# Mean squares of a mixer step's input: from token-major tiles with ACT accumulators instead of folds over feature-major squares

## The chip, the cores and the metric

One core of a Trainium2 chip runs the whole step. The metric is device microseconds (us) of one execution, the median of three runs. Engines are called as the profile calls them: PE (TensorE), DVE (VectorE), ACT (ScalarE), POOL (GpSimd), SP (SyncE, which here only issues transfers).

## The reference

One decoder layer over 2,112 tokens (2,048 of a prompt, 64 of samples) with 1,024 features, in float32. What bears on the change is the norm and the projection ahead of everything:

```python
def rms_norm(x, g):
    y = xf * lax.rsqrt(jnp.mean(xf * xf, axis=-1, keepdims=True) + NORM_EPS)
    return (y * g.astype(jnp.float32)).astype(x.dtype)
...
    xn = rms_norm(x, norm_pre)
    z = jnp.einsum('btd,de->bte', xn, w_in.astype(xn.dtype))
    v_pool = z[:, :, 0:W_POOL]
    g_pool = z[:, :, W_POOL:2 * W_POOL]
    ...
    y_pool, new_pool = pool_mixer(v_pool, pool_buf, start_pos, pool_w, pool_scale)
```

So each token needs one number, the reciprocal root of the mean square of its 1,024 features. After that come a pooling mixer with a gate, a convolution with a gated linear recurrence and its gate, an output projection, a second norm and the residual.

## The kernel before, in words

Tokens are cut into five chunks of up to 426 columns (`CHUNKS`; c = 0 to 4). The normalised input of all chunks stays in SBUF, features on partitions (feature-major): eight blocks k of 128 features, W columns each, as a high part `xh` and a low part `xl`, both rounded to fp32r. A projection of a chunk (`z_k`) is three matmuls for each k: high weights by `xh`, high weights by `xl`, low weights by `xh`.

The change is in the first stage, pool group 0, which runs under `tc.manual_schedule()` (L596 to L812): each engine takes its instructions in the order in which the code writes them. For every chunk PE computes two value blocks (v0, v1), the group's linear map of the chunk before (`pool_mm`) and two gate blocks (g0, g1), 24 + 24 + 12 + 24 + 24 matmuls. The last chunk has 12 more for its own map; then `fold_mm` starts the next stage.

Chunk 0 is the odd one: its matmuls run on x times the norm's gain (`x_g`, `x_hi`, `x_lo`), and the reciprocal root `r0` comes in afterwards, where DVE takes v0 and v1 out of PSUM (`pool_evac`) and g0 and g1 (L717). For chunks 1 to 4 `normalise` multiplies x in place by gain and root (DVE, L239), ACT rounds the high part (L247) and DVE or POOL subtracts for the low part (L256).

Where the roots come from: ACT squares x feature-major (`square`, L583; L675 for chunk 4, whose blocks are loaded for it in passing and loaded again by `normalise`), `fold` adds the eight blocks of features by halving (4, 2, 1 blocks; on DVE for chunks 0 and 1, on POOL for 2 and 3; `add_parts` on POOL for chunk 4), and one matmul of a 128x128 matrix of ones (`mean_sq`, L211) sums over the partitions and spreads the sum to all of them. ACT takes Ln and Exp (`rsqrt_table`), DVE makes a Newton step on 128 x W elements (`rsqrt_newton`), and the row `r` lies in SBUF. `MS0_AT`, `MS1_AT` and `MS_AT` say behind which k that matmul stands in PE's order. Ln and Exp share a table of ACT that Silu isn't in, so the code loads tables by hand.

All transfers go through SP's queue, in order. SBUF slots of 128 x 3,408 float32 (tag `xn`, ten of them) hold x, `xh`, `xl`, staged weights and the squares.

Of the kernel before, what the change touches and what calls it, by code (L numbers as in the profile page):

```python
# [61 lines left out]
def hymba_kernel(  # L62
# [146 lines left out]
    def mean_sq(c, acc):  # L209
        ms = s_psum(f"ms{c}")[:, :XR[c][1] - XR[c][0]]  # L210
        nc.tensor.matmul(ms, lhsT=ones, rhs=acc, start=True, stop=True)  # L211
        return ms

    def rsqrt_table(ms, r, preload=True):
        if preload:
# [4 lines left out]
    def rsqrt_newton(acc, ms, r):  # L220
        V = nc.vector
        V.scalar_tensor_tensor(out=acc, in0=ms, scalar=D * EPS, in1=r, op0=ALU.add, op1=ALU.mult)
        V.scalar_tensor_tensor(out=acc, in0=acc, scalar=-0.5 / D, in1=r, op0=ALU.mult, op1=ALU.mult)
        V.scalar_tensor_tensor(out=r, in0=acc, scalar=1.5, in1=r, op0=ALU.add, op1=ALU.mult)
# [355 lines left out]
    sqt = {}  # L580

    def square(c, k0, k1):
        A.activation(out=sqt[c][:, k0 * CW:k1 * CW], in_=xraw[c][:, k0 * CW:k1 * CW], func=AF.Square)  # L583

    def fold(c, eng, acc, ns):
        W = XR[c][1] - XR[c][0]
        for n in ns:
            eng.tensor_tensor(out=sqt[c][:, 0:n * W] if n > 1 else acc, in0=sqt[c][:, 0:n * W],
                              in1=sqt[c][:, n * W:2 * n * W], op=ALU.add)
# [6 lines left out]
    with tc.manual_schedule():  # L596
# [55 lines left out]
        square(0, 6, 8)
        acc0 = t_tile("xa0")[:, :CW]
        acc1 = t_tile("xa1")[:, :CW]
        fold(0, V, acc0, (4, 2, 1))
# [2 lines left out]
        square(1, 0, 4)
        square(1, 4, 8)
        half = 2 * CW  # L660
        for eng, o in ((G, 0), (V, half)):
            eng.tensor_tensor(out=sqt[1][:, o:o + half], in0=sqt[1][:, o:o + half],
                              in1=sqt[1][:, 2 * half + o:3 * half + o], op=ALU.add)
        fold(1, V, acc1, (2, 1))
# [3 lines left out]
        def squares(c):
            sqt[c] = half_slot(f"sq{c}", F32)
            square(c, 0, 4)  # L670
            square(c, 4, 8)

        def square_part(k):
            t = x_part(LAST, k)
            A.activation(out=t, in_=t, func=AF.Square)  # L675
            return t
# [828 lines left out]
```

## Time and profile before

| | |
|---|---|
| median of three runs | 1207.81 us (1207.54 to 1207.96) |
| the profiled execution | 1207.61 us, its span 1205.7 us |
| PE busy | 1169.7 us, 97% of the span |
| DVE, ACT, POOL busy | 869.0, 556.0, 391.8 us |
| mean granted clock of PE | 0.991 |
| PE busy in the first four of 40 slices (30 us each), tenths | 6, 8, 8, 7; from the fifth on 9 nearly throughout |

PE works nearly without a break, apart from the first 150 us and the last few. The profile therefore has to be read in the first stage: where PE waits there, for whom, and why that one was late. Times in the rows further down are us from the start of the span.

### The profile page before, as it was taken

How to read it: one execution, taken by the hardware profiler on the slowest of the kernel's cores; microseconds unless marked ns; L12 is line 12 of the kernel's file. 1: busy time of each engine (PE TensorE's matmuls, PEld its weight loads, DVE VectorE, ACT ScalarE, POOL GpSimd, SP SyncE). 2: the span in 40 equal slices, each digit the busy share in tenths (PEclk: the TensorE clock that was granted, in tenths of full speed). 3: DMA queues.
4: the chain of work that ended last, by engine and by line, in shares of the span. 5: the costliest groups of instructions: out<-in, count | busy, mean ns of one | idle time of the engine just before them, and what ended most of it. 6: DMA issues, size and time to landing. Idle time of an engine off the chain costs nothing.

```text
span 1205.7 us, 16176 instructions
## 1 busy us (share of the span) xinstructions
PE 1169.7 (97%) x5762; PEld 1075.1 (89%) x5762; DVE 869.0 (72%) x1209; ACT 556.0 (46%) x986; POOL 391.8 (32%) x498
## 2 busy tenths in 40 slices
PE   6887999999999999999999999999999999999997
PEld 5787999999999999999999999999978878888886
DVE  7899654435545455888888888889976678888687
ACT  5464321221221125676767676677754333344232
POOL 4466530341251152333333334334320002221242
PEclk9899999999999999999999999999999999999999
DMA  9011362543341020111111111112469857767553
GB/s 320 21 44 57 93 211 93 166 141 118 120 159 57 28 62 32 53 43 43 47 37 44 40 53 48 44 40 84 141 196 275 249 168 206 224 190 236 158 164 140
DMA packets 126673, 140.02 MB, mean 116 GB/s; under 512 B 12288, under 2 KB 88320, under 8 KB 126592
## 3 DMA queue, kind: packets, MB, share of 16 engines
q1 hardware_dynamic: 126592, 138.99, 37.7%
q8 instruction: 45, 0.74, 0.3%
q14 instruction: 36, 0.29, 0.1%
HBM read 99.46 MB, written 39.24 MB: 115 GB/s over the span
## 4 chain that ended last, share of the span: by engine, by line
PE 72%; DVE 11%; DMA 8%; ACT 5%; POOL 2%; issue 2%; SPq 0%; DVEq 0%; ACTq 0%; POOLq 0%
PE p L995 6%; PE p L994 6%; PE p L993 6%; PE u L269 5%; PE u L270 5%; PE u L271 5%; PE lg L269 5%; PE lg L270 4%; PE lg L271 4%; PE v L269 3%; PE v L270 3%; PE v L271 3%; PE g L269 3%; PE g L271 3%; PE g L270 3%; DMA a<-mixed 3%
## 5 line engine op out<-in xcount | busy, mean ns | idle before, releaser
L471 DVE SCALAR_TENSOR_TENSOR xs<-u,parT,xs 128x426 f32<-128x426 f32 (+1 forms) x120 | 108.9, 907 | 46.9 <-ACT xs L467 30.7
L270 PE MATMUL v<-xl,w 128*128 128x426 f32 (+2 forms) x320 | 117.7, 368 | 11.0 <-DVE xl L256 8.7
L269 PE MATMUL v<-xh,w 128*128 128x426 f32 (+2 forms) x320 | 118.5, 370 | 7.8 <-ACT xh L574 7.4
L986 POOL TENSOR_TENSOR xr<-ac,xr 128x512 f32<-128x512 f32 x28 | 47.2, 1707 | 230.2 <-DVE ac L1124 126.4
L269 PE MATMUL g<-xh,w 128*128 128x426 f32 (+1 forms) x320 | 115.5, 361 | 3.8 <-ACT e L303 3.8
L271 PE MATMUL v<-xh,w 128*128 128x426 f32 (+2 forms) x320 | 114.5, 363 | 0.0
L269 PE MATMUL u<-xh,w 128*128 128x426 f32 (+1 forms) x320 | 114.0, 356 | 0.0
L270 PE MATMUL g<-xl,w 128*128 128x426 f32 (+1 forms) x320 | 114.0, 356 | 0.0
L271 PE MATMUL g<-xh,w 128*128 128x426 f32 (+1 forms) x320 | 113.9, 356 | 0.1
L269 PE MATMUL lg<-xh,w 128*128 128x426 f32 (+1 forms) x320 | 113.9, 356 | 0.0
L270 PE MATMUL lg<-xl,w 128*128 128x426 f32 (+1 forms) x320 | 113.4, 354 | 0.0
L270 PE MATMUL u<-xl,w 128*128 128x426 f32 (+1 forms) x320 | 113.4, 354 | 0.0
L271 PE MATMUL lg<-xh,w 128*128 128x426 f32 (+1 forms) x320 | 113.4, 354 | 0.0
L271 PE MATMUL u<-xh,w 128*128 128x426 f32 (+1 forms) x320 | 113.2, 354 | 0.0
L1286 DVE RECIPROCAL rv<-rv 128x426 f32<-128x426 f32 (+1 forms) x40 | 112.4, 2811 | 0.0
L993 PE MATMUL p<-ws,s 128*128 128x512 f32 (+1 forms) x264 | 102.3, 387 | 0.7 <-ACT s L106 0.7
L994 PE MATMUL p<-ws,s 128*128 128x512 f32 (+1 forms) x264 | 102.2, 387 | 0.2 <-DVE ws L109 0.2
L995 PE MATMUL p<-ws,s 128*128 128x512 f32 (+1 forms) x264 | 102.3, 388 | 0.0
L270 PEld LDWEIGHTS v<-xl,w 128*128 128x128 f32 x320 | 62.0, 194 | 17.9 <-DVE xl L256 11.3
L994 PE MATMUL p<-ws,a 128*128 128x512 f32 x192 | 75.8, 395 | 0.5 <-DVE ws L109 0.4
L993 PE MATMUL p<-ws,a 128*128 128x512 f32 x192 | 75.7, 394 | 0.5 <-ACT ws L106 0.5
L332 DVE TENSOR_TENSOR s<-e 128x440 f32<-128x440 f32 (+3 forms) x40 | 30.9, 771 | 62.7 <-ACT e L303 49.0
(235 smaller groups left out, 2891.7 us busy)
## 6 DMA issues: line engine op xcount, KB each, us to landing
a<-mixed SPq DMA_DIRECT2D x112, 256.0 KB, 4.3
wr<-in_w_in SPq DMA_DIRECT2D x56, 256.0 KB, 3.1
wo<-in_w_out SPq DMA_DIRECT2D x32, 256.0 KB, 3.8
wtd<-wo SPq DMA_DIRECT2D x32, 256.0 KB, 2.3
w<-wtd SPq DMA_DIRECT2D x32, 256.0 KB, 3.8
xr<-in_x SPq DMA_DIRECT2D x32, 256.0 KB, 3.7
out<-xr SPq DMA_DIRECT2D x30, 256.0 KB, 2.6
mixed<-sg SPq DMA_DIRECT2D x32, 213.0 KB, 2.0
```

Source lines behind the costliest of these rows:

```text
L269: nc.tensor.matmul(out, lhsT=wh, rhs=xh, start=(k == 0), stop=False)
L270: nc.tensor.matmul(out, lhsT=wh, rhs=xl, start=False, stop=False)
L271: nc.tensor.matmul(out, lhsT=wl, rhs=xh, start=False, stop=(k == KT - 1))
L332: nc.vector.tensor_tensor(out=dst[:, first:L], in0=src[:, first:L], in1=src[:, first - sh:L - sh], op=ALU.add)
L471: nc.vector.scalar_tensor_tensor(out=xs, in0=E[:, k:k + n], scalar=col(C_CW + 8 * k, b), in1=xs, op0=ALU.mult, op1=ALU.add)
L986: (eng or nc.vector).tensor_tensor(out=out, in0=a, in1=b, op=op)
L993: nc.tensor.matmul(out, lhsT=ah, rhs=wh, start=start and k == 0, stop=False)
L994: nc.tensor.matmul(out, lhsT=ah, rhs=wl, start=False, stop=False)
L995: nc.tensor.matmul(out, lhsT=al, rhs=wh, start=False, stop=stop and k == KT - 1)
L1286: nc.vector.reciprocal(out=v, in_=v)
```

## The change

x is loaded a second time, token-major: 17 tiles of 128 tokens x 1,024 features (512 KB each, the last one half), three to a slot. ACT squares a tile in place with an accumulator (`tok_square`), which gives the sum of a token's squares in one column of the small tile `tok`. `tok_rsqrt` makes root columns out of sums for several tiles at once (7, 3 and 7 columns): mean and epsilon on DVE, Ln and Exp on ACT, a Newton step on DVE, all on 128 x 3 or 128 x 7 elements. `r_rows` turns the columns of a chunk into a row on all partitions: for each of the four or five tiles that the chunk touches ACT scales columns of an identity matrix by the root column (a diagonal `dg`), and a matmul of ones with it writes the piece into PSUM. There `normalise` reads it; only r0 is copied to SBUF. `R01_AT` and `R_AT` place these matmuls in PE's order. The squares, folds, `add_parts`, the first loads of chunk 4 and all but one table load for Ln go.

```diff
@@ rows of roots
+    tok = sb.tile([P, 3, N_TT], F32, name="tok")
+    def load_tok(i, slot):
+        lo, hi = i * P, min((i + 1) * P, T_ALL)
+        t = tok_box[i] = slot[:hi - lo, i % 3 * D:(i % 3 + 1) * D]
+        nc.sync.dma_start(out=t, in_=x[lo:hi, :])
+    def tok_square(i):
+        t = tok_box[i]
+        nc.scalar.activation(out=t, in_=t, func=AF.Square, accum_out=tok[:t.shape[0], 0, i:i + 1])
+    def tok_rsqrt(i0, i1):
+        V = nc.vector
+        ms, u, r = (tok[:, i, i0:i1] for i in range(3))
+        V.tensor_scalar(out=ms, in0=ms, scalar1=1.0 / D, scalar2=EPS, op0=ALU.mult, op1=ALU.add)
+        nc.scalar.activation(out=r, in_=ms, func=AF.Ln)
         nc.scalar.activation(out=r, in_=r, func=AF.Exp, scale=-0.5)
+        V.tensor_tensor(out=u, in0=ms, in1=r, op=ALU.mult)
+        V.scalar_tensor_tensor(out=u, in0=u, scalar=-0.5, in1=r, op0=ALU.mult, op1=ALU.mult)
+        V.scalar_tensor_tensor(out=r, in0=u, scalar=1.5, in1=r, op0=ALU.add, op1=ALU.mult)
+    def r_rows(c):
+        lo, hi = XR[c]
+        dg = tp_tile(f"dg{c}")
+        R = s_psum(f"r{c}")[:, :hi - lo]
+        for i in range(lo // P, (hi - 1) // P + 1):
+            n = min(P, T_ALL - i * P)
+            a, b = max(lo, i * P), min(hi, i * P + n)
+            nc.scalar.activation(out=dg[:n, a - lo:b - lo], in_=ident[:n, a - i * P:b - i * P], func=AF.Copy,
+                                 scale=tok[:n, 2, i:i + 1])
+            nc.tensor.matmul(R[:, a - lo:b - lo], lhsT=ones[:n, :], rhs=dg[:n, a - lo:b - lo], start=True, stop=True)
+        return R
...
@@ opening: loads
         stage_w(8, 0, 2)
+        for i in range(4):
+            load_tok(i, slots[i // 3])
         load_x(1, 0, 4)
+        for i in range(4, 6):
+            load_tok(i, slots[1])
         load_x(1, 4, 8)
+        load_tok(6, slots[2])
...
@@ opening: ACT, PE and DVE (the squares of chunks 0 and 1 and their folds go)
         w_hi(8, 0, A)
         w_lo(8, 0, G)
+        for i in range(3):
+            tok_square(i)
         w_hi(8, 1, A)
         w_lo(8, 1, G)
+        for i in range(3, 7):
+            tok_square(i)
+        for i in range(7, 9):
+            load_tok(i, slots[2])
         load_x(3, 0, KT)
...
-            if k == MS0_AT:
-                ms0 = mean_sq(0, acc0)
-        rsqrt_table(ms0, r0, False)
-        rsqrt_newton(acc0, ms0, r0)
+        for i in range(9, 12):
+            load_tok(i, slots[1])
+        tok_rsqrt(0, 7)
...
         for k in range(KT):
+            if k == R01_AT:
+                R0, r1 = r_rows(0), r_rows(1)
+                A.copy(out=r0, in_=R0)
             z_k(Z0[3], wt[9], 0, k)
...
-        squares(2)
...
-        accs = {2: sums(2, G)}
-        normalise(1, r1, [V])
+        normalise(1, r1, [V], {3: (7,), 5: (8,), 7: (9,)})
+        for i in range(10, 12):
+            tok_square(i)
+        for i in range(12, 15):
+            load_tok(i, slots[2])
...
@@ chunks 1 to 4
-                r = rsqrt()
+                tok_rsqrt(7, 10)
+                r = r_rows(n)
...
-                squares(3)
-                accs[3] = sums(3, G)
...
-                    if k == MS_AT and n:
-                        r = rsqrt()
+                    if k == R_AT and n:
+                        r = r_rows(n)
...
-                    add_parts()
-                    parts = [square_part(k) for k in range(4, KT)]
-                    add_parts()
...
-                last = normalise(n, r, LO_ENGS[n], SQUARES if c == 1 else {})
+                last = normalise(n, r, LO_ENGS[n], {1: (12,), 3: (13,), 5: (14,)} if c == 1 else {})
             if c == 1:
+                for i in range(15, 17):
+                    load_tok(i, slots[2])
+                    tok_square(i)
+                tok_rsqrt(10, 17)
                 silus()
...
-                nc.scalar.preload_act_table_set("natural_log_exp_and_others")
```

The numbers behind a name tell its buffers apart. Three places show how the order on the engines changes.

SP's queue at the opening, before and then now, from the load of weight block 8 (`wst`, 128x1024) on. `xr_123` and `xr_134` are x of chunk 1, `xr_131` and `xr_144` of chunk 2, `xr_192` and `xr_199` of chunk 3, `w9r` is weight block 9; `tok_108`, `tok_109`, `tok_110` are the three slots of token-major tiles.

```order
L556 DMA wst<-in_w_in 128x1024
L198 DMA xr_123<-in_xt 128x4x426 x2
L611 DMA w9r_91<-in_w_in 128x512
L611 DMA w9r_92<-in_w_in 128x512
L615 DMA pw0r<-in_pool_w 128x512
L198 DMA xr_131<-in_xt 128x8x426
L198 DMA xr_192<-in_xt 128x8x426
```

```order
L578 DMA wst<-in_w_in 128x1024
L220 DMA tok_108<-in_x 128x1024 x3
L220 DMA tok_109<-in_x 128x1024
L202 DMA xr_134<-in_xt 128x4x426
L220 DMA tok_109<-in_x 128x1024 x2
L202 DMA xr_134<-in_xt 128x4x426
L220 DMA tok_110<-in_x 128x1024
L627 DMA w9r_96<-in_w_in 128x512
L627 DMA w9r_97<-in_w_in 128x512
L629 DMA pw0r<-in_pool_w 128x512
L202 DMA xr_144<-in_xt 128x8x426
```

Seven token-major tiles (0 to 6) now stand among and behind the loads of chunk 1 and ahead of weight block 9; tiles 7 to 11 follow chunks 2 and 3.

ACT at the opening, from the cast of weight block 8's first half to the first cast of chunk 1 (`xh_326`, now `xh_341`), before and then now. `w_0_99`, `w_1_100` and now `w_0_104`, `w_1_105` are the two halves of weight block 9.

```order
L562 CAST w_0_97<-wst 128x512
L583 ACTIVATE sq_128<-xr_123 128x1704 x2
L562 CAST w_1_98<-wst 128x512
L217 ACTIVATE r_104<-ms_239,epsT 128x426
L218 ACTIVATE r_104<-r_104 128x426
L562 CAST w_0_99<-w9r_91 128x512
L562 CAST w_1_100<-w9r_92 128x512
L217 ACTIVATE xr_279<-ms_267,epsT 128x426
L218 ACTIVATE xr_279<-xr_279 128x426
L583 ACTIVATE sq_319<-xr_131 128x1704 x2
L247 CAST xh_326<-xr_123 128x426 x2
```

```order
L224 ACTIVATE tok_109,tok<-tok_109 128x1024 x3
L224 ACTIVATE tok_110,tok<-tok_110 128x1024
L230 ACTIVATE tok<-tok 128x7
L231 ACTIVATE tok<-tok 128x7
L584 CAST w_0_104<-w9r_96 128x512
L584 CAST w_1_105<-w9r_97 128x512
L243 ACTIVATE dg_295<-ident,tok 128x128 x3
L243 ACTIVATE dg_295<-ident,tok 128x42
L243 ACTIVATE dg_305<-ident,tok 128x86
L243 ACTIVATE dg_305<-ident,tok 128x128 x2
L243 ACTIVATE dg_305<-ident,tok 128x84
L691 COPY r_111<-r_296 128x426
```

The casts of weight block 9 now stand behind the squares of tiles 0 to 6 and the roots of seven columns; before they stood behind the roots of chunk 0.

ACT in chunk 3, around the roots of chunk 4, before and then now. `xh_101` and `xh_106` are the high parts of chunk 0, which is normalised anew there for the other pool groups.

```order
L805 ACT_TABLE_LOAD
L247 CAST xh_101<-xr_112 128x852 x4
L217 ACTIVATE xr_809<-ms_807,epsT 128x424
L218 ACTIVATE xr_809<-xr_809 128x424
L303 COPY e_3_815<-v_3_781 128x426
L760 ACT_TABLE_LOAD
```

```order
L269 CAST xh_106<-xr_119 128x852 x4
L243 ACTIVATE dg_813<-ident,tok 128x104
L243 ACTIVATE dg_813<-ident,tok 128x128 x2
L243 ACTIVATE dg_813<-ident,tok 64x64
L325 COPY e_3_823<-v_3_787 128x426
```

Before, PE's matmul `ms_807` stood ahead of ACT's work and needed only sums from POOL; now PE's matmuls for chunk 4's row need these four diagonals, which ACT makes behind the four casts.

## Rows read from the trace of the kernel before

**Rows 1.** The waits of PE in the first 165 us: who waited for whom; us in total, how often, longest.

```profile
PE v L270 <- DVE xl L256: 8.7, 4, 3.1
...
PE g L269 <- ACT e L303: 3.8, 1, 3.8
PE ms L211 <- DVE xa L588: 3.3, 1, 3.3
PE v L270 <- POOL xl L256: 1.5, 2, 0.9
...
PE y L284 <- POOL dl L109: 0.7, 1, 0.7
PE f L285 <- POOL wtl L109: 0.5, 1, 0.5
```

**Rows 2.** PE's timeline in the first stage, the matmuls at which blocks begin or waits end: start, duration, line, operation, and in brackets the idle time before it and who ended it. The row of 53.75 is the sum for chunk 2, the next one the start of `pool_mm`; the rows of 66.10, 93.20 and 123.68 begin chunks 2, 3 and 4, the last one the next stage.

```profile
24.05 1.79 PE L211 MATMUL ms<-xa,ones 128*128 128x426 f32 x2 [3.34 <-DVE xa L588]
...
53.75 0.88 PE L211 MATMUL ms<-xa,ones 128*128 128x426 f32 x2
...
59.10 0.35 PE L283 MATMUL y<-dh,pw 128*128 128x426 f32 x1
...
61.44 0.36 PE L269 MATMUL g<-xh,w 128*128 128x426 f32 x1
...
66.10 0.36 PE L269 MATMUL v<-xh,w 128*128 128x426 f32 x1
...
70.91 0.46 PE L270 MATMUL v<-xl,w 128*128 128x426 f32 x1 [3.10 <-DVE xl L256]
...
93.20 0.36 PE L269 MATMUL v<-xh,w 128*128 128x426 f32 x1
...
123.68 0.35 PE L269 MATMUL v<-xh,w 128*128 128x408 f32 x1
...
147.39 0.28 PE L283 MATMUL f<-pw,wth 128*128 128x256 f32 x1
```

**Rows 3.** Stretches of 10 us in the first stage: busy time of PE and its instructions, granted clock of PE (1.00 is 2.4 GHz), share of the DMA engines, GB/s.

```profile
20.00:30.00 10.00, 6.66 (x25) 0.83 0.93 333
40.00:50.00 10.00, 7.79 (x28) 0.66 0.00 0
...
70.00:80.00 10.00, 9.03 (x36) 0.83 0.12 44
90.00:100.00 10.00, 7.86 (x37) 1.00 0.00 0
110.00:120.00 10.00, 7.02 (x30) 0.83 0.11 25
```

**Rows 4.** DVE's timeline between 36 and 110 us, columns as in rows 2.

```profile
36.14 3.84 DVE L256 TENSOR_TENSOR xl<-xr,xh 128x426 fp32r<-128x426 f32 x1 [0.37 <-issue]
39.90 3.66 DVE L239 SCALAR_TENSOR_TENSOR xr<-xr,parT,xr 128x426 f32<-128x426 f32 x2
43.48 0.59 DVE L256 TENSOR_TENSOR xl<-xr,xh 128x426 fp32r<-128x426 f32 x1
...
49.26 1.10 DVE L717 TENSOR_TENSOR sg<-g,r 128x426 f32<-128x426 f32 x2
...
54.03 0.16 DVE L358 TENSOR_TENSOR d<-df,e 128x1 f32<-128x1 f32 x1
...
59.30 2.38 DVE L239 SCALAR_TENSOR_TENSOR xr<-xr,parT,xr 128x426 f32<-128x426 f32 x4
62.04 4.28 DVE L256 TENSOR_TENSOR xl<-xr,xh 128x852 fp32r<-128x852 f32 x1 [0.35 <-ACT xh L247]
...
92.73 4.13 DVE L239 SCALAR_TENSOR_TENSOR xr<-xr,parT,xr 128x426 f32<-128x426 f32 x4
...
101.71 8.78 DVE L239 SCALAR_TENSOR_TENSOR xr<-xr,parT,r 128x426 f32<-128x426 f32 x8
```

**Rows 5.** POOL's timeline in the same time, columns as in rows 2.

```profile
27.68 2.90 POOL L565 TENSOR_TENSOR w<-w9r,w 128x512 fp32r<-128x512 f32 x2 [2.56 <-ACT w L562]
...
35.70 6.14 POOL L588 TENSOR_TENSOR sq<-sq 128x1704 f32<-128x1704 f32 x2 [3.25 <-ACT sq L583]
...
48.86 1.63 POOL L109 TENSOR_TENSOR pw<-pw0r,pw 128x512 fp32r<-128x512 f32 x1 [5.76 <-ACT pw L106]
...
92.87 2.38 POOL L256 TENSOR_TENSOR xl<-xr,xh 128x852 fp32r<-128x852 f32 x1
```

**Rows 6.** The transfers of the first 60 us: GB/s in 40 slices of 1.5 us, and a group of issues (four loads of 212 KB each into an idle queue) with its median time from issue to landing in us.

```profile
GB/s 0 179 315 191 345 322 352 424 393 394 379 381 382 380 382 379 382 379 362 84 137 156 0 0 0 5 0 0 0 0 0 0 0 0 139 6 0 0 0 0
...
x<-in_xt SPq DMA_DIRECT2D x4, 212.0 KB, 2.6
```

**Rows 7.** ACT's groups of instructions by line and shape over the whole program: count, busy us, mean ns of one, idle time before them and what ended it.

```profile
L583 ACT ACTIVATE sq<-xr 128x1704 f32<-128x1704 f32 x6 | 9.4, 1621 | 0.0
...
L1104 ACT ACTIVATION_READ_ACCUMULATOR p<-ac 128x1 f32 x33 | 6.2, 187 | 0.0
...
L583 ACT ACTIVATE sq<-xr 128x852 f32<-128x852 f32 x4 | 3.5, 906 | 0.0
...
L310 ACT COPY e<-v 128x64 f32<-128x64 f32 x8 | 1.8, 223 | 0.0
...
L562 ACT CAST w<-w9r 128x512 fp32r<-128x512 f32 x2 | 1.1, 610 | 0.0
```

More of the change, by code (lines that the diff above doesn't have):

```diff
@@ L55 @@
 LATE = 544
-MS0_AT = 9
-MS1_AT = 5
-MS_AT = 7
+R01_AT = 3
+R_AT = 7
+N_TT = (T_ALL + P - 1) // P
 @with_exitstack
@@ L122, in hymba_kernel @@
     epsT, neg1 = epsT[:, 0:1], epsT[:, 1:2]
+    ident = sb.tile([P, P], F32, name="ident")
+    nc.gpsimd.memset(ident, 1.0)
+    nc.gpsimd.affine_select(out=ident, in_=ident, pattern=[[-1, P]], compare_op=ALU.is_equal, fill=0.0,
+                            base=0, channel_multiplier=1)
     rcnt = sb.tile([P, PB], F32, name="rcnt")
@@ L207, in x_part @@
         return t
[L209 to L215, printed above, removed]
-            nc.scalar.preload_act_table_set("natural_log_exp_and_others")
-        nc.scalar.activation(out=r, in_=ms, func=AF.Ln, scale=1.0 / D, bias=epsT)
-        nc.scalar.activation(out=r, in_=r, func=AF.Exp, scale=-0.5)
[L220 to L224, printed above, removed]
+    tok = sb.tile([P, 3, N_TT], F32, name="tok")
@@ L248, in normalise @@
                 for j in squares.get(k, ()):
-                    parts.append(square_part(j))
+                    tok_square(j)
                 lo()
@@ L578, in x_lo @@
         eng.tensor_tensor(out=xn[0][1][:, p], in0=xg[k], in1=xn[0][0][:, p].bitcast(F32), op=ALU.subtract)
[L580 to L589, printed above, removed]
     xn[0] = half_slot("xh0", F32R), half_slot("xl0", F32R)
-    sqt[0] = half_slot("sq0", F32)
+    slots = [half_slot(f"tok{i}", F32) for i in range(3)]
     r0 = sb.tile([P, LATE], F32, tag="late", bufs=1, name="r0")[:, :CW]
@@ L624, in hymba_kernel @@
         x_lo(1, G)
-        square(0, 0, 2)
         w_hi(1, 0, V)
@@ L635, in hymba_kernel @@
         w_lo(0, 1, V)
-        square(0, 2, 4)
         x_g(4)
@@ L648, in hymba_kernel @@
         x_hi(7)
-        square(0, 4, 6)
         x_lo(6, V)
         x_lo(7, V)
[L652 to L655, printed above, removed]
         w_hi(8, 0, A)
         w_lo(8, 0, G)
[L658 to L664, printed above, removed]
+        for i in range(3):
+            tok_square(i)
         w_hi(8, 1, A)
         w_lo(8, 1, G)
[L668 to L676, printed above, removed]
+        for i in range(3, 7):
+            tok_square(i)
+        for i in range(7, 9):
+            load_tok(i, slots[2])
         load_x(3, 0, KT)
@@ L695, in hymba_kernel @@
             w_lo(9, h, G)
-        r1 = t_tile("xr1")[:, :CW]
-        rsqrt_table(ms1, r1, False)
+        for k in range(KT):
+            if k == R01_AT:
+                R0, r1 = r_rows(0), r_rows(1)
+                A.copy(out=r0, in_=R0)
+            z_k(Z0[3], wt[9], 0, k)
         Es, sgs0 = [], []
@@ L701, in hymba_kernel @@
             Es.append(E)
-        rsqrt_newton(acc1, ms1, r1)
-        for k in range(KT):
-            z_k(Z0[3], wt[9], 0, k)
-        squares(2)
-        def sums(c, eng):
-            acc = t_tile(f"xa{c}")[:, :XR[c][1] - XR[c][0]]
-            fold(c, eng, acc, (4, 2, 1))
-            return acc
-        accs = {2: sums(2, G)}
-        normalise(1, r1, [V])
+        normalise(1, r1, [V], {3: (7,), 5: (8,), 7: (9,)})
[3 more added lines that the diff above has]
+            load_tok(i, slots[2])
         pw0 = split_small(pw0r, 512, "pw0")
@@ L723, in hymba_kernel @@
         prev = prevE0
-        parts = []
-        SQUARES = {3: (0, 1), 5: (2, 3)}
-        def add_parts():
-            if LAST not in accs:
-                accs[LAST] = t_tile(f"xa{LAST}")[:, :XR[LAST][1] - XR[LAST][0]]
-                G.tensor_tensor(out=accs[LAST], in0=parts.pop(0), in1=parts.pop(0), op=ALU.add)
-            while parts:
-                G.tensor_tensor(out=accs[LAST], in0=accs[LAST], in1=parts.pop(0), op=ALU.add)
         LO_ENGS = {2: [V], 3: [V, G, V, G], 4: [V, G]}
```

14 lines of the change are left out of this document (2 added, 12 removed).

## The prediction

> **What bounds it now.** PE is busy nearly throughout, so I read first for whom it waits, then what each block costs it, then why the one waited for was late. The waits of PE [rows 1] are nearly all in the first stage: 8.7 us for low parts from DVE, 3.8 for an evacuation on ACT, 3.3 for the sum of chunk 0, 1.5 for low parts from POOL, and 0.7 and 0.5 at the stage's end. A block of 24 matmuls without a wait lasts from 61.44 to 66.10, 4.66 us; the 5.35 us from 53.75 to 59.10 hold such a block and one sum, so the sum is 0.69 us [rows 2]. A middle chunk has 108 matmuls and one sum: 4.5 x 4.66 + 0.69 = 21.66 us. Chunk 2 took 27.10 us and chunk 3 took 30.48 [rows 2]: 5.4 and 8.8 too much. In chunk 2, 3.10 of this is one wait. The rest is mostly clock: behind waits of 2.7 us and more the granted clock falls, and a 10 us stretch at 0.83 is a third of its time at 1.2 GHz, 3.3 us, in which PE does half, so 1.7 us lost; at 0.66 it is 3.4 us [rows 3].
>
> Why are the low parts late? One low part of 426 columns took 3.84 us at 36.14 and 0.59 at 43.48; two scalings took 3.66 at 39.90, four took 2.38 at 59.30 [rows 4]. All this time POOL folds squares (6.14 us from 35.70) [rows 5], and so again at 62.04. DVE is held up beside POOL, not overloaded. In chunk 3 the reason is a queue: DVE normalises chunk 0 anew until 101.71 + 8.78 = 110.49 [rows 4], ACT rounds behind it, and only then come the roots and the evacuation for which PE waits 3.8 us [rows 1].
>
> **The opening: a wait goes, another comes.** PE's 3.3 us wait for the sum [rows 1] goes: PE is free at 24.05 - 3.34 = 20.7 [rows 2], and the 27 matmuls up to the end of g0 take 5.2 us: 25.9. But weight block 9, which g1 needs, is now cast behind tiles 0 to 6. Up to tile 6 SP asks for 8.77 MB (weights 1.57, chunks 0 and 1 3.49, seven tiles 3.67, parameters 0.04); before, the burst of 9.38 MB (four chunks 6.98, weights 2.10, pool weights 0.26, parameters) ended at 28.5 and ran at about 380 GB/s [rows 6]. The last byte of tile 6 thus comes 0.61 MB / 380 GB/s = 1.6 us earlier, at 26.9. A load of 212 KB takes 2.6 us in an idle queue, 0.6 of it bytes; I put half of the other 2.0 behind the last byte: landing at 27.9. The fastest slice (424) would give 1.5 us less, the slower landing 1 more.
>
> A square of 1,024 columns lies between the 852 and 1,704 forms (0.91 and 1.62 us): 1.05, and with the accumulator's read (0.19) about 1.1 pipelined [rows 7]. So 29.0. Three tiny steps (DVE 0.16 [rows 4], ACT twice 0.22 [rows 7], handoffs 0.3) end at 29.9, the cast (0.61 [rows 7]) at 30.5, POOL's low part (1.45 each [rows 5]) at 31.95. PE idles 4.6 us, does two matmuls, waits 0.7 more, and runs at the lower clock: seven matmuls in 2.5 us, 34.45. By then the eight diagonals are done (0.22 us by the 64-column form, 0.61 by the 512-column one [rows 7]; 128 columns lie near the lower end, at 0.28, and I take 0.35 for the scale column that they read). Both rows cost 2 x 0.69, r0's being out at 35.15; the other 15 matmuls end at 38.75. r0's copy takes 0.5, the two evacuations 1.10 as those at 49.26, so `normalise` of chunk 1 starts at 36.75. Unhindered it takes 8.7 us: the 5.8 from 43.48 to 49.26 plus four scalings (2.38) and a short low part (0.59) [rows 4]. No POOL work of any length is beside it now. PE's third pair of blocks waits for its low part until 42.5; the values end at 49.5. Before, that was 53.75 [rows 2].
>
> **The next wait: chunk 2's row.** It stands in PE's order ahead of g0 of chunk 1, and its columns behind DVE's gate products and windows and ACT's casts for them. From 49.26 to 54.19 DVE took 4.93 us for this [rows 4]; now from 45.5, so 50.4. Root columns: 0.9 to the Exp, 0.7 for three tiny DVE steps, 1.4 for four diagonals: the row is complete at 53.5, after an idle time near 3 us. Then 60 matmuls (11.65) and one low-clock stretch (1.7): chunk 2 starts at 66.9 instead of 66.10, **0.8 us later**. Two thirds of what the opening won is given back here.
>
> **Chunks 2 to 4.** `normalise` of chunk 2 runs from 53.5 to about 63, so the wait of 3.10 us and its clock go: **-5.4 us**. POOL's folds and partial sums go too; SP gets to chunk 4's blocks early, since only tiles and stores stand ahead. Chunk 3 keeps a queue: ACT casts chunk 0 anew ahead of the diagonals for chunk 4's row. Counted from chunk 2's start T: v0 and its evacuation 5.2, a window's two steps 1.2, four scalings 2.4, a low part 1.0, four scalings 2.4, then as before from 96.86 (the end of 92.73 + 4.13) to 110.49, 13.6 [rows 4]: T + 25.8. A cast of 852 columns (0.9) and four diagonals (1.4) give T + 28.1, the row T + 28.2. PE would have it at T + 21.66 + 4.66 + 0.69 = T + 27.0, so 1.2 us of wait come in; I take it as too short for the clock, as chunk 3's own waits, none over 0.9 [rows 1], left it at 1.00 from 90 to 100 [rows 3]. Chunk 3 costs 8.8 - 1.2 less: **-7.6 us**. The banks of g0 are free by then. In chunk 4 the waits of 0.7 and 0.5 [rows 1] should go, as DVE's windows and stores come earlier than PE: **-1.2 us**. From there on PE is full and all moves forward alike. Table loads saved on ACT and the Newton steps saved on DVE count nothing by themselves; they are cover that grows.
>
> The second four scalings of chunk 3 are where row and rule part. At 92.73 four of them took 4.13 us while POOL ran a low part (2.38 at 92.87 [rows 5]); I took 2.4, because their root row is now in PSUM, and the two products at 49.26, one input from PSUM, took 1.10 us beside POOL's 1.63 from 48.86 [rows 4, 5]. The Trainium skill (SBUF — State Buffer, Who interferes with whom) says that a DVE instruction with at most one SBUF input, outside the two-port modes, doesn't contend with GpSimd. By it the sum is as given; by the row at 92.73 it is the second rival.
>
> **Sum.** +0.8 - 5.4 - 7.6 - 1.2 = -13.4 us on the profiled execution's 1207.61 (the median of the runs is 0.20 above it): **1194.2 us**.
>
> **Rivals.**
> 1. Scalings with a row in PSUM are held up by POOL all the same. Chunk 4's row comes 1.75 us later, PE's wait is 3 us, and the clock falls (1.7): 3.4 lost, **1197.6 us**. For it: 92.73. Against: 49.26.
> 2. The two new waits before chunk 2 are longer: tiles 7 to 11 land later, or small steps cost more with their handoffs, or the clock stays low through both. Half of the terms 0.9 + 0.7 + 1.4 again, 1 us of landing and another 1.7 us of clock: **1198.4 us**. For it: chains of tiny steps across engines don't occur in this stage before. Against: the burst shows no slow slice [rows 6].
> 3. DVE's slowness isn't POOL's doing, and the low parts come as late as before: only chunk 3's evacuation (3.8 and 1.7 of clock) and -1.2 are won, the opening loses what it gains: **1201 us**. Against: 43.48 beside 36.14.
> 4. Slower: the squares of tiles 9 to 11 stand in ACT's queue ahead of all that chunk 2's row needs. Tile 11 is byte 15.66 MB of the burst, 12.3 MB behind the first weights and chunk 0, which are through at 12.4 us. At 380 GB/s it lands near 46, in time. At 230 GB/s it lands at 67; square, pool weights, two casts, then the 3 us of small steps give a row at 73 instead of 53.5, 19.5 us later: **1213.7 us**. It decides from about 260 GB/s down. Against: from the eighth slice to the nineteenth none is below 362 [rows 6]; a transfer of 4 KB rows with tiles being waited for isn't in them.
>
> **Chances.** Forecast 0.54, rival 1 0.16, rival 2 0.17, rival 3 0.04, rival 4 0.05; 0.04 for no effect at all. Range: downward, tile 6 1.5 us earlier and one low-clock stretch less (1.7), 1191.0; upward rivals 1 and 2 and 0.7 us each of restarts left in chunks 2 to 4, short of rival 4: 1202.5. The forecast's own range is 1191.0 to 1197. This kernel's measurement tells about 0.2% (2.4 us) from no change: faster 0.91, same 0.04, slower 0.05.
>
> **What would show it.** Right: low parts of chunk 1 and 2 at 0.6 and 1.0 us; PE's longest waits near 26 us for ACT's cast of weight block 9 and near 50 us for ACT's diagonal; chunk 2 starting near 67, chunk 3 near 88.6, chunk 4 near 111.5, the next stage near 134.5; a wait near 1 us for the diagonal in chunk 3. Wrong: a wait of over 3 us there (rival 1), tile 6 squared after 31 us or chunk 2 starting after 70 (rival 2), DVE low parts of 3 us without POOL beside them (rival 3), ACT idle for a transfer near 50 us (rival 4).

## The result and the profile after

| | before | after |
|---|---|---|
| median of 10 runs each | 1207.67 us | 1201.57 us |
| ratio, 95% interval | | 0.9949 [0.993, 0.9967] |
| profiled execution's span | 1205.7 us | 1198.7 us |
| chunk 2 starts (forecast 66.9) | 66.10 | 70.15 |
| chunk 3 starts (88.6) | 93.20 | 92.27 |
| chunk 4 starts (111.5) | 123.68 | 119.74 |
| next stage starts (134.5) | 147.39 | 142.09 |

The kernel is faster by 0.5%, about 6 us, where 13.4 us were forecast: inside the stated range, but 7.3 us short of the forecast. By term: opening +4.05 us (forecast +0.8), chunk 2 -4.98 (-5.4), chunk 3 -3.01 (-7.6), chunk 4 -1.36 (-1.2 with the stage's end), and what follows -1.70. The two large errors, 3.25 and 4.6 us, are the subject below.

The waits of PE in the first 165 us, the answer to [rows 1]; us in total, how often, longest. The waits of before are gone: of the 8.7 us for low parts 0.6 is left, and nothing of the 3.8 us for the evacuation and the 3.3 us for the sum. (The first and the fourth line lie in the opening 20 us, which the change leaves alone.) New are three waits for ACT's diagonals, 7.4 us, and one for block 9's weights, 3.1 us.

```profile
PE v L291 <- ACT xh L596: 7.5, 2, 6.1
PE r L245 <- ACT dg L243: 7.4, 3, 3.3
PE g L291 <- ACT w L584: 3.1, 1, 3.1
PE v L292 <- DVE xl L600: 0.7, 2, 0.6
PE v L292 <- DVE xl L278: 0.6, 1, 0.6
PE g L293 <- POOL w L587: 0.3, 1, 0.3
```

PE's timeline, the answer to [rows 2]: start, duration, instruction, idle time before it and who ended it. `r` is a row of roots. The row of 53.78 is chunk 2's, that of 100.41 chunk 4's; 70.15, 92.27 and 119.74 begin chunks 2 to 4.

```profile
30.32 0.72 PE L291 MATMUL g<-xh,w 128*128 128x426 f32 x1 [3.15 <-ACT w L584]
...
34.32 3.07 PE L245 MATMUL r<-dg,ones 128*128 128x128 f32 x16
37.18 0.44 PE L291 MATMUL g<-xh,w 128*128 128x426 f32 x1
...
40.18 0.35 PE L291 MATMUL v<-xh,w 128*128 128x426 f32 x1
...
53.78 0.65 PE L245 MATMUL r<-dg,ones 128*128 128x44 f32 x2 [3.29 <-ACT dg L243]
55.22 1.65 PE L245 MATMUL r<-dg,ones 128*128 128x128 f32 x6 [0.79 <-ACT dg L243]
56.52 0.70 PE L291 MATMUL g<-xh,w 128*128 128x426 f32 x1
...
70.15 0.36 PE L291 MATMUL v<-xh,w 128*128 128x426 f32 x1
...
92.27 0.35 PE L291 MATMUL v<-xh,w 128*128 128x426 f32 x1
...
100.41 1.56 PE L245 MATMUL r<-dg,ones 128*128 128x104 f32 x8 [3.32 <-ACT dg L243]
...
119.74 0.35 PE L291 MATMUL v<-xh,w 128*128 128x408 f32 x1
```

The stretches of 10 us, PE alone (busy us and instructions, granted clock, DMA share, GB/s; [rows 3] of before). The clock falls behind each of the long waits: 0.66, 0.69 and 0.83.

```profile
30.00:40.00 10.00, 9.41 (x40) 0.66 1.05 390
...
50.00:60.00 10.00, 5.93 (x21) 0.69 0.01 2
...
90.00:100.00 10.00, 7.09 (x37) 1.00 0.42 130
100.00:110.00 10.00, 9.59 (x42) 0.83 0.00 0
```

DVE's timeline ([rows 4] of before). The low parts of chunk 1 take 0.60, the first one of chunk 2 1.04 us where before had 3.84 and 4.28: the mechanism of the forecast. At 83.11 four scalings with the row in PSUM take 2.36 us, though POOL computes low parts beside them (83.00, 2.09 us); [rows 4] had 4.13. What to look at is the bracket of 82.15. POOL's own rows stand below.

```profile
39.02 0.60 DVE L278 TENSOR_TENSOR xl<-xr,xh 128x426 fp32r<-128x426 f32 x1
...
49.51 1.57 DVE L362 SCALAR_TENSOR_TENSOR d<-s,e 128x426 f32<-128x426 f32 x1
51.00 1.03 DVE L379 TENSOR_TENSOR df<-s,rcnt 128x1 f32<-128x1 f32 x1
...
59.19 1.04 DVE L278 TENSOR_TENSOR xl<-xr,xh 128x852 fp32r<-128x852 f32 x1
...
76.80 2.36 DVE L261 SCALAR_TENSOR_TENSOR xr<-xr,parT,r 128x426 f32<-128x426 f32 x4
82.15 1.05 DVE L278 TENSOR_TENSOR xl<-xr,xh 128x852 fp32r<-128x852 f32 x1 [3.00 <-ACT xh L269]
83.11 2.36 DVE L261 SCALAR_TENSOR_TENSOR xr<-xr,parT,r 128x426 f32<-128x426 f32 x4
...
90.35 8.79 DVE L261 SCALAR_TENSOR_TENSOR xr<-xr,parT,r 128x426 f32<-128x426 f32 x8
```

```profile
49.17 1.45 POOL L109 TENSOR_TENSOR pw<-pw0r,pw 128x512 fp32r<-128x512 f32 x1 [11.12 <-ACT pw L106]
50.58 1.44 POOL L109 TENSOR_TENSOR dl<-d,dh 128x426 fp32r<-128x426 f32 x1
...
83.00 2.09 POOL L278 TENSOR_TENSOR xl<-xr,xh 128x852 fp32r<-128x852 f32 x1 [1.43 <-ACT xh L269]
```

ACT's timeline around the two late rows. ACT works strictly in its own order: the diagonals of 53.41 and 54.77 come behind the casts of `pw` and `dh`; and in chunk 2 the evacuation `e` of 80.79 waits 3.33 us for PE's second value, with the casts `xh` of 81.20 queued behind it.

```profile
27.92 1.06 ACT L224 ACTIVATE tok<-tok 128x1024 f32<-128x1024 f32 x1 [2.37 <-DMA tok<-in_x]
28.89 0.19 ACT L224 ACTIVATION_READ_ACCUMULATOR tok<-tok 128x1 f32 x1
...
48.49 0.60 ACT L106 CAST pw<-pw0r 128x512 fp32r<-128x512 f32 x1
...
52.62 0.55 ACT L106 CAST dh<-d 128x426 fp32r<-128x426 f32 x1 [3.07 <-DVE tok L229]
...
53.41 0.32 ACT L243 ACTIVATE dg<-ident,tok 128x44 f32<-128x44 f32 x1
54.77 0.98 ACT L243 ACTIVATE dg<-ident,tok 128x128 f32<-128x128 f32 x3 [1.04 <-DVE tok L234]
...
80.79 0.52 ACT L325 COPY e<-v 128x426 f32<-128x426 f32 x1 [3.33 <-PE v L293]
81.20 1.71 ACT L269 CAST xh<-xr 128x852 fp32r<-128x852 f32 x2
...
99.17 0.90 ACT L269 CAST xh<-xr 128x852 fp32r<-128x852 f32 x1 [0.24 <-DVE xr L261]
99.98 1.20 ACT L243 ACTIVATE dg<-ident,tok 128x104 f32<-128x104 f32 x4
```

### The profile page after: what moved, and what is told of

The parts are those of the page before. It is cut to its first block, busy times and chain, and to the rows that moved or that the text cites. A ratio compares the mean times of both kernels' runs of the same rounds, so it can differ in the third digit from the quotient of the medians.

```text
span 1198.7 us, 16264 instructions
## 1 busy us (share of the span) xinstructions
PE 1169.1 (98%) x5794; PEld 1079.4 (90%) x5794; DVE 829.1 (69%) x1201; ACT 552.3 (46%) x1015; POOL 356.5 (30%) x486
## 4 chain that ended last, share of the span: by engine, by line
PE 77%; DVE 8%; DMA 6%; ACT 3%; issue 2%; POOL 1%; SPq 0%; DVEq 0%; ACTq 0%; POOLq 0%
PE p L964 6%; PE p L963 6%; PE p L962 6%; PE u L291 5%; PE u L293 5%; PE u L292 5%; PE lg L291 5%; PE lg L292 4%; PE lg L293 4%; PE v L291 4%; PE v L293 4%; PE v L292 4%; PE g L291 4%; PE g L293 4%; PE g L292 4%; DMA a<-mixed 3%
## 5 line engine op out<-in xcount | busy, mean ns | idle before, releaser
L493 DVE SCALAR_TENSOR_TENSOR xs<-u,parT,xs 128x426 f32<-128x426 f32 (+1 forms) x120 | 109.4, 911 | 46.1 <-ACT xs L489 30.5
L291 PE MATMUL v<-xh,w 128*128 128x426 f32 (+2 forms) x320 | 116.7, 365 | 7.9 <-ACT xh L596 7.5
L293 PE MATMUL v<-xh,w 128*128 128x426 f32 (+2 forms) x320 | 113.7, 360 | 0.0
L962 PE MATMUL p<-ws,a 128*128 128x512 f32 x192 | 75.7, 394 | 1.0 <-ACT ws L106 1.0
L964 PE MATMUL p<-ws,a 128*128 128x512 f32 x192 | 75.8, 395 | 0.8 <-DVE a L109 0.8
L963 PE MATMUL p<-ws,a 128*128 128x512 f32 x192 | 75.7, 394 | 0.4 <-DVE ws L109 0.4
L354 DVE TENSOR_TENSOR s<-e 128x440 f32<-128x440 f32 (+3 forms) x40 | 29.2, 730 | 66.9 <-ACT e L325 48.2
```

Source lines behind the costliest of these rows:

```text
L291: nc.tensor.matmul(out, lhsT=wh, rhs=xh, start=(k == 0), stop=False)
L293: nc.tensor.matmul(out, lhsT=wl, rhs=xh, start=False, stop=(k == KT - 1))
L354: nc.vector.tensor_tensor(out=dst[:, first:L], in0=src[:, first:L], in1=src[:, first - sh:L - sh], op=ALU.add)
L493: nc.vector.scalar_tensor_tensor(out=xs, in0=E[:, k:k + n], scalar=col(C_CW + 8 * k, b), in1=xs, op0=ALU.mult, op1=ALU.add)
L962: nc.tensor.matmul(out, lhsT=ah, rhs=wh, start=start and k == 0, stop=False)
L963: nc.tensor.matmul(out, lhsT=ah, rhs=wl, start=False, stop=False)
```

## The experiments

Theory: what the change removes is won as forecast, and the missing part is lost in two places, at chunk 2's row and at chunk 4's, because of ACT's order and for no other reason. Rivals: DVE is late anyhow, or POOL or the transfers are behind it. All ratios are against the kernel before on the same chip; the changed kernel's is 0.9949, and 0.001 is 1.2 us. The diffs leave out the split of `r_rows` into `r_diag` (ACT) and `r_mm` (PE), and line numbers shift by some 10 from it.

**Chunk 4's row earlier.**

```
             if c == 2:
+                r4 = r_rows(4)
                 normalise(0, r0, [G])
...
                     if k == R_AT and n:
-                        r = r_rows(n)
+                        r = r4 if c == 3 else r_rows(n)
```

> One step is moved: the two diagonals and the matmuls of ones that make chunk 4's row of reciprocal roots are issued at the end of chunk 2's pass (behind its second gate's matmuls, ahead of the scalings of the pass over chunk 0), no longer in the middle of chunk 3's pass. Theory (TensorE waits in chunk 3 because ScalarE is in order: the diagonals stand behind the casts of the pass over chunk 0, these behind VectorE's scalings, these behind ScalarE's evacuation of chunk 2's second value): the wait of 3.32 us at 100.4 us and the low clock behind it (about 1.7 us) are gone, chunk 3 lasts 22.0 to 23.0 us where the changed kernel has 27.47, chunk 2's start stays at 70.2 +- 0.3, and the span is 4 to 5 us under 1198.7 (a time near 1196.5). Rival (VectorE is late in any case, because POOL's subtractions or the row in PSUM hold it): a wait of 2 to 4 us for the scalings or low parts of chunk 4 turns up in chunk 3 or at chunk 4's start (119.7 - 4.9 = 114.8 by the theory, 117 or later by the rival), and the time moves by 2 us or less.

Measured: 1196.87 us, 0.9901 [0.9879, 0.9922]. Chunk 3 lasts from 90.55 to 112.78, 22.23 us, and PE waits for nobody in it; the row costs it only its own matmuls. So the 5.2 us of chunk 3 are the wait and its clock, and nothing else was late: the rival would have put a wait for scalings in its place. One figure missed: chunk 2 starts at 68.43, not 70.2, as the clock came back sooner in the opening (see the last section). At the next stage, 135.13, the kernel is thus 7.0 us ahead of the changed one; the profiled execution's span is 3.9 us shorter.

**Chunk 2's row earlier.**

```
         normalise(1, r1, [V], {3: (7,), 5: (8,), 7: (9,)})
+        tok_rsqrt(7, 10)
+        d2 = r_diag(2)
         for i in range(10, 12):
             tok_square(i)
...
-                tok_rsqrt(7, 10)
-                r = r_rows(n)
+                r = r_mm(n, d2)
```

> The roots of tiles 7 to 9 and chunk 2's diagonals are issued right behind the normalisation of chunk 1, ahead of ScalarE's squares of tiles 10 and 11, of the cast of the pool weights and of the casts of the window differences; the matmuls of the row stay at their place. Theory (the 4.1 us by which chunk 2 starts late come from ScalarE's order): TensorE's waits for the diagonals (3.29 and 0.79 us at 53.8 to 55.2) and the low clock in the first gate of chunk 1 (about 2 us) are gone, and chunk 2 starts between 63.5 and 66.0 us instead of 70.15. The silus and dh casts then stand between chunk 3's squares and its diagonals, so TensorE may wait 1 to 3 us for chunk 3's diagonals in chunk 2. Chunk 4's wait (3.3 us, in chunk 3) stays. Time 3 to 5 us below the changed kernel, about 1197. Rival (VectorE's normalisation of chunk 2 or its transfers are what comes late): chunk 2 starts at 68.5 us or later, TensorE waiting for low parts of chunk 2 instead.

Measured: 1196.01 us, 0.989 [0.9866, 0.9915]. The wait is gone, chunk 2 starts at 62.84 and the next stage at 134.81, both 7.3 us earlier than in the changed kernel, more than the 4.1 to 6.7 expected. The feared wait for chunk 3's diagonals did not come. But the profiled execution's span is only 4.1 us shorter: of the 7.3 us some 3 are missing behind that point, 1.7 of them in one new wait for the weights of a fold in the next stages (`wth`, none in the changed kernel). How much of the rest is spread is open: two executions of the changed kernel differ by 1.1 us in that stretch. By the ratio the time is 7.1 us lower, where 3 to 5 were expected.

**Both, and chunk 3's diagonals ahead of the silus.**

```
                 tok_rsqrt(10, 17)
+                d3 = r_diag(3)
                 silus()
```

> Both moves, and chunk 3's diagonals issued ahead of the silus: no row of reciprocal roots is waited for any more behind chunk 1's start. Theory: chunk 2 starts at 63.5 to 66 us, chunks 2, 3 and 4 last 22.0 to 23.0 us each, the next stage begins at 130 to 133 us (142.1 in the changed kernel), and the time is 9 to 12 us below the changed kernel, 1189.5 to 1192.5. By the rivals of the two single moves (VectorE late for other reasons) the waits come back under VectorE's name and the time is 1195 or more. The two single moves add up if the theory holds: the gain of this one is the sum of theirs within 2 us, and up to 3 us more for chunk 3's diagonals.

Measured: 1191.11 us, 0.985 [0.9829, 0.9871], inside the forecast range. Chunk 2 and the next stage start earlier than expected (62.22 for 63.5 to 66, 128.92 for 130 to 133). No row is waited for; PE's rows with their marks:

```profile
49.69 1.05 PE L252 MATMUL r<-dg,ones 128*128 128x44 f32 x8
...
62.22 0.36 PE L301 MATMUL v<-xh,w 128*128 128x426 f32 x1
...
84.34 1.19 PE L252 MATMUL r<-dg,ones 128*128 128x104 f32 x8
...
128.92 0.28 PE L315 MATMUL f<-pw,wth 128*128 128x256 f32 x1
```

The next stage starts 13.2 us before the changed kernel's; by the ratio the time is 12 us lower. The two single moves make 5.8 and 7.1 us by their ratios, 12.9 together. So both waits for late rows hang on the order of ACT's queue, at two places. About 1 us of the opening's error has another cause (the dearer rows of the second failed step below).

**POOL's work put back.** Was DVE's old slowness POOL's doing at all (rival 3 of the prediction)? Six additions of 426 columns have as many columns as POOL's two longest folds of before together (1,704 and 852).

```
+        junk = tp_tile("junk1")[:, :CW]
+        for i in range(6):
+            G.tensor_tensor(out=junk, in0=xraw[2][:, i * CW:(i + 1) * CW],
+                            in1=xraw[2][:, (i + 1) * CW:(i + 2) * CW], op=ALU.add)
         normalise(1, r1, [V], {3: (7,), 5: (8,), 7: (9,)})
... (the same with xraw[3] beside normalise(2))
```

> The changed kernel with six additions of 426 columns (SBUF with SBUF, result in a tile that nobody reads) put back on POOL beside each of the normalisations of chunks 1 and 2, where before had POOL's folds of squares. Nothing else differs. Theory (VectorE's low parts and scalings took 3.7 to 4.3 us in before because POOL worked on two SBUF operands beside them): low parts of chunk 1 and 2 that lie beside the additions take 3 to 4.5 us again (0.60 to 1.04 in the changed kernel), scalings that read the row from PSUM keep their 1.1 to 1.2 us (2.37 in the view's pairs), TensorE waits 3 to 8 us more for low parts of chunk 1 and 2 up to 75 us, and the time rises by 3 to 9 us, to 1204 to 1210. Rival (VectorE was slow in before because it also squared or because of what lay in its queue, not because of POOL): low parts stay under 1.3 us, and the time rises by 1 us at most.

Measured: 1203.69 us, 0.9956 [0.994, 0.9972]: hardly a cost, against the expectation of 3 to 9 us. In the trace chunk 2 starts 1.0 us and the next stage 2.4 us later than in the changed kernel. DVE's timeline, with POOL's 6.52 us of additions running from 37.86:

```profile
37.56 1.22 DVE L261 SCALAR_TENSOR_TENSOR xr<-xr,parT,r 128x426 f32<-128x426 f32 x2
38.89 1.39 DVE L278 TENSOR_TENSOR xl<-xr,xh 128x426 fp32r<-128x426 f32 x1
...
41.34 1.23 DVE L278 TENSOR_TENSOR xl<-xr,xh 128x426 fp32r<-128x426 f32 x1
```

A low part beside the additions loses 0.4 to 0.8 us, not 3, in both chunks; the scalings lose nothing. So neither side of the expectation holds in full: the low parts, 1.23 to 1.66 us, lie between its rival's 1.3 and its theory's 3 us. Two explanations stood open: POOL's instructions are shorter here (426 columns against 1,704), or the scalings, whose row is in PSUM, now slip past.

**Before, with short folds.** The kernel before, each of POOL's folds cut into pieces of 426 columns.

```
         for n in ns:
+            for i in range(n) if eng is G else (None,):
+                a, b = (0, n * W) if i is None else (i * W, (i + 1) * W)
... (the addition on columns a to b)
```

> The kernel before, with each of POOL's folds of squares cut into pieces of 426 columns (1704 into four additions, 852 into two): same data, same columns, same engine, only shorter instructions. In before, VectorE's low part beside the 1704-column fold lasted 3.84 us and its two scalings beside the 852-column fold 3.66 us; with six 426-column additions of POOL put into the changed kernel the low parts beside them lasted 1.23 to 1.66 us. Theory A (VectorE stands still until POOL's running instruction ends, so the price goes by the length of one instruction): VectorE's first low part of chunk 1 lasts 1.2 to 1.7 us (3.84 before) and chunk 2's 1.4 to 2.0 us (4.28 before), TensorE's waits for low parts of chunks 1 and 2 (2.70, 2.18 and 3.10 us) fall to under 1.5 us each and 3.5 us in total or less, chunk 2 starts 2 to 5 us earlier than 66.1 us, and the time is 3 to 8 us below before. Theory B (the price goes by the columns that POOL works through): low parts and scalings are stretched as much in total, the waits stay at 7 to 8 us in total, and the time stays within 2 us of before or rises.

Measured: 1208.01 us, 1.0003 [0.9992, 1.0013]. A is right on the single instruction and B on the time. DVE's timeline beside POOL's pieces (8.14 us from 36.53):

```profile
36.97 1.12 DVE L256 TENSOR_TENSOR xl<-xr,xh 128x426 fp32r<-128x426 f32 x1 [0.37 <-issue]
38.01 2.89 DVE L239 SCALAR_TENSOR_TENSOR xr<-xr,parT,xr 128x426 f32<-128x426 f32 x2
40.83 1.48 DVE L256 TENSOR_TENSOR xl<-xr,xh 128x426 fp32r<-128x426 f32 x1
...
45.05 1.78 DVE L256 TENSOR_TENSOR xl<-xr,xh 128x852 fp32r<-128x852 f32 x1
```

The first low part is down from 3.84 to 1.12 us, but every instruction now loses a piece. From the first low part to the end of the first wide one it is 9.86 us here and 10.03 in before (from 36.14 to 45.14 + 1.03). Short folds help nothing, which leaves the scalings, whose row lies in SBUF here.

**The row's place, chunk 3.**

```
                         r = r_rows(n)
+                        if n == 3:
+                            R3, r = r, t_tile("r3")[:, :CW]
+                            A.copy(out=r, in_=R3)
```

> The changed kernel, with chunk 3's row of reciprocal roots copied from PSUM into SBUF by ScalarE and the scalings of chunk 3 reading that copy. Nothing else differs. Theory (a scaling with one operand in PSUM is not held up by POOL's subtractions, one with both operands in SBUF is): the four scalings beside POOL's first low part of chunk 3 take 3.9 to 4.6 us instead of 2.36 us (4.13 us in before), the later steps of VectorE up to chunk 4's row come 1.5 to 2.5 us later, TensorE's wait in chunk 3 grows from 3.3 us by 1 to 2.5 us, and the time rises by 1 to 3 us. Rival (the row's place does not matter, what mattered was the folds alone): the four scalings stay at 2.3 to 2.5 us, the time within 1 us.

Measured: 1206.53 us, 0.998 [0.9967, 0.9992]: 3.7 us lost of the 6, more than expected. Four scalings take 5.00 us, for 2.36 with the row in PSUM; PE's wait in chunk 3 grows from 3.32 to 6.18. POOL's rows below show that its subtraction `dl` fell beside these scalings here (in the changed kernel it came ahead of them, at 77.60). They thus met more of POOL's work than there, and part of the 5.00 us is owed to that.

```profile
83.04 5.00 DVE L261 SCALAR_TENSOR_TENSOR xr<-xr,parT,r 128x426 f32<-128x426 f32 x4
87.97 1.03 DVE L278 TENSOR_TENSOR xl<-xr,xh 128x852 fp32r<-128x852 f32 x1
```

```profile
82.42 1.67 POOL L109 TENSOR_TENSOR dl<-d,dh 128x426 fp32r<-128x426 f32 x1 [5.19 <-PE y L306]
...
85.14 2.44 POOL L278 TENSOR_TENSOR xl<-xr,xh 128x852 fp32r<-128x852 f32 x1
```

**Folds and place, chunks 1 and 2.** Three kernels on one chip: the changed one once more, one with both rows copied to SBUF, one with the copies and POOL's additions.

```
+                R1, r1 = r1, t_tile("r1s")[:, :CW]
+                A.copy(out=r1, in_=R1)
... (r2s for chunk 2 alike; the additions as above)
```

> The changed kernel itself once more, as the mark for the two kernels beside it and for the repeat of its waits: 0.9949 of the time before (0.993 to 0.997), chunk 2 at 70.2 us and the next stage at 142.1 us, each within 1.5 us; waits for diagonals of 3.3 us ahead of chunk 2's row and of chunk 4's row.

> The changed kernel with the rows of chunks 1 and 2 copied by ScalarE from PSUM to SBUF (0.52 us each), so that the scalings of chunks 1 and 2 have both operands in SBUF; POOL has nothing of any length beside them. Theory (the row's place only matters beside POOL's work): two scalings last 1.2 us and four 2.4 us as before the edit, chunk 2 starts within 1 us of the changed kernel's start, and the time is within 1.5 us of it. Rival (a scaling with its row in SBUF is slower by itself): a pair lasts 1.4 us or more, and chunk 2 starts 1.5 us later or more.

> The same copies of the rows to SBUF, and beside the normalisations of chunks 1 and 2 six additions of 426 columns on POOL each, whose result nobody reads. Theory (both are needed for the old slowness: POOL working on SBUF, and scalings whose operands all lie in SBUF): a pair of scalings beside the additions lasts 2.5 to 3.0 us (1.22 us with the same additions and the row in PSUM; 2.89 us where the kernel before had its folds cut to 426 columns), TensorE waits 4 to 6 us in total for low parts of chunk 1 (2.2 us with the row in PSUM), chunk 2 starts at 73 to 76 us (71.1), and the time is 3 to 8 us above the kernel with the additions and the row in PSUM, which was 0.9956 of before: 1206 to 1212. Rival (the additions alone made their whole cost already): pairs stay under 1.5 us, chunk 2 starts at 71 to 72.5 us, time within 1.5 us of that kernel.

| chunks 1 and 2 | row in PSUM | row in SBUF |
|---|---|---|
| POOL idle beside DVE | 0.9946 [0.993, 0.9961] | 0.9942 [0.9917, 0.9966] |
| six additions on POOL | 0.9956 [0.994, 0.9972] | 0.9988 [0.9968, 1.0008] |

(The lower left is the run of POOL's work put back, above.) Neither edit alone costs what a measurement can tell; both together cost 5 us (0.9988 against 0.9946). The two intervals of the lower line still touch, so the traces have to bear it out. From chunk 1's first scaling to chunk 3's start it is 54.6 us in the changed kernel, 53.7 with the row in SBUF, 55.7 with the additions and 59.0 with both: the additions cost 1.1 us with the row in PSUM and 5.3 with it in SBUF. DVE's pair of scalings beside the additions, with the row in SBUF, is back at 2.59 us:

```profile
38.98 2.59 DVE L261 SCALAR_TENSOR_TENSOR xr<-xr,parT,r1s 128x426 f32<-128x426 f32 x2
```

The time, 1207.53 us, fell into the range expected. Chunk 2's start, 71.71 instead of 73 to 76, did not: PE's waits for low parts rose to 4.2 us as expected, but the wait for the diagonals shrank from 3.29 to 1.00, since the one delay hides part of the other. Two limits: the profiled execution is the fastest of the ten (1203.38 us), and chunk 2's old wait of 3.10 us for a low part is not back in it (chunk 2 lasts 23.9 us, 1.29 of them a wait for chunk 3's diagonals, against 22.1 in the changed kernel and 27.1 in before). The kernel with the rows in SBUF alone missed one figure, chunk 2's start, 1.6 us before the changed kernel's instead of within 1; its opening was the quicker one (see the last section).

**A better kernel.** All rows early as above, and block 9's weights loaded and cast earlier.

```
+        for h in range(2):
+            nc.sync.dma_start(out=w9r[h], in_=w_in[9, :, 512 * h:512 * (h + 1)])
         load_tok(6, slots[2])
+        load_x(1, 4, 8)
... (each moved up or down from its neighbours; w_hi(9), w_lo(9) ahead of tok_square(6);
     r_rows(0), r_rows(1) behind the second gate of chunk 0)
```

> The kernel with all rows issued early (1191.11 us), and in addition: block 9's weights are loaded ahead of tile 6 and of the second half of chunk 1's raw x, cast ahead of the square of tile 6, and the rows of chunks 0 and 1 are issued behind the second gate of chunk 0 instead of in its middle. Theory (the wait for block 9's weights, 3.44 us at 26.9 us, and the low clock in the rows behind it, some 1 us, are of the order of the transfers and of ScalarE's queue): TensorE's wait before the second gate is 0 to 0.8 us, the rows of chunks 0 and 1 are done between 33.0 and 34.5 us, the values of chunk 1 start at 36.0 to 37.5 us (39.13), a wait of 1.5 to 3 us for the first high part of chunk 1 takes the place of part of the old one, chunk 2 starts at 59.5 to 61 us (62.22), and the time is 1.5 to 3 us lower, 1188 to 1189.6 us. Rival (roots of chunks 0 to 1 or the landing of tile 6 set the end there, not the weights): the values of chunk 1 start at 38.5 us or later, and the time stays within 0.7 us of 1191.1.

Measured: 1186.63 us, 0.9827 [0.9807, 0.9847], 1.7% below before. PE works through from 20 to 30 us (10.00 us busy at clock 1.00), waits 1.96 us for the first high part, and starts chunk 1's values at 35.55 and chunk 2 at 60.05. At the next stage it is 2.2 us ahead of the kernel with all rows early. That is the gain shown, as the intervals of the two times overlap (0.9847 and 0.9829). The span is 4.9 us shorter, so 2.7 came behind that point, where its waits of PE are 3.0 us instead of 4.9. That part I had not expected; the time lies below the 1188 to 1189.6 us expected.

## Why the prediction was wrong

**Right.** Tile 6 was squared at 27.92 (forecast 27.9) in 1.06 + 0.19 us, PE got the weights at 30.32 (30.5), low parts took 0.60 and 1.04 us, and chunk 2 gave -4.98 for -5.4. The transfers kept pace (390 GB/s to 40 us): rival 4 was not near. The waits stand at the two places named, and chunk 4's term held.

**Luck.** The time lies inside the range because its upper end adds the prices of rivals 1 and 2 (3.4 and 4.2 us). What was lost is near their sum, but for the most part not in the ways that they describe. Nor does the time speak for rival 3, whose number, 1201 us, it nearly hits: the low parts of 3 us that rival 3 asks for are not there.

**Step 1 that failed: chunk 3, -7.6.** The count from chunk 2's start T read "v0 and its evacuation 5.2, a window's two steps 1.2, four scalings 2.4, a low part 1.0". The low part needs ACT's cast, and ACT's cast stands behind the evacuation of chunk 2's *second* value, which the count left out. DVE thus stands still for 3.00 us at 82.15, which is T + 12.0 instead of T + 8.8. The rest of the count was right to the tenth: from 82.15 to the end of the pass over chunk 0, 99.14, it is 17.0 us, as forecast (1.0 + 2.4 + 13.6). So PE's wait was 3.32 us, not 1.2. (It grew by 2.1 us and not by 3.2, as PE starts with the first diagonal, at 100.41, where the count waits for the fourth.) Behind it the granted clock was 0.83 (from 100 to 110), a loss that the sum had put at nothing. Chunk 3 was thus 3.01 us shorter instead of 7.6. Moving the row gave 5.2 us back; the order of evacuation and casts was not changed in any run, so its 3.00 us are read from the rows. The wait that rival 1 foresaw came, by a way that none of the rivals described: the scalings themselves were not held up (2.36 us at 83.11).

**Step 2 that failed: the opening, +0.8.** Chunk 2 started 3.25 us later than forecast. About 1 us came from the two rows of chunks 0 and 1: priced at 0.69 us each, they took 2.86 together (34.32 to 37.18), as PE was still at its lower clock (0.66 from 30 to 40), and `normalise` of chunk 1 began at 37.70, not 36.75. Another 2 us lie in the chain to chunk 2's row, where I summed each engine's own steps and let them hand over at once. POOL's subtraction for the pool weights and one for a window (49.17 and 50.58) fell on DVE's window steps (1.57 for 0.60, 1.03 for 0.15); the 4.93 us taken over from before held one such delay, not two. ACT's second `dh` cast went ahead of Ln; the row was complete at 56.5, not 53.5. Moving the diagonals up took this chain away, and more. It is rival 2's case, and its sign, chunk 2 after 70, is there; but it came by the small steps, ACT's order and the clock, not by late transfers.

**Right for half the reason.** I gave the gain in chunks 1 and 2 to POOL's lost folds alone. The table above speaks for the row in PSUM doing nearly the same with POOL's work left in: the two are cures for one illness, and their gains don't add. This is shown with additions of 426 columns; folds of 1,704 columns beside a row in PSUM were not run. In chunk 3, where POOL still works beside DVE, the row's place is worth 3.7 us. The rule that I had weighed decided it: the Trainium skill (SBUF — State Buffer, Who interferes with whom) exempts a DVE instruction with at most one SBUF input, outside the two-port modes, from contention with GpSimd. The traces agree: beside the same additions a pair of scalings took 1.22 us with the row in PSUM and 2.59 with it in SBUF.

**Slips in the text of the prediction.** "The second rival" of the row at 92.73 is rival 1. By its own figures the opening wins 4.25 us (the values end at 49.5 for 53.75) and chunk 2 starts 0.8 us late, so all of it is given back, not two thirds. The range's upper end adds 0.7 us once, not for each of three chunks. None of the three touches the forecast's sum.

## What to carry to other kernels

When a wait is removed, follow the next consumer's operands through every in-order queue they cross, instruction by instruction; here ACT had an evacuation that waited for PE ahead of casts that DVE needed, and chunk 3 won 3.01 us where 7.6 were forecast. Small producers of something needed soon (here four diagonals, 1.2 us) belong ahead of bulk work on the same engine, as far ahead as their inputs allow. And before crediting a gain to the part that was removed, test the parts crosswise: two parts of a change can each remove the same cost.
